# Attention's masked scores in the buffers of the recurrence's key and query copies, the output parts and their turned form in one block product buffer

## The chip, the cores and the metric

The kernel runs on one core of one Trainium2 chip. The metric is the device time of one execution in microseconds (us). The executions of the kernel before took 1199.67, 1202.01 and 1202.31 us; their median is 1202.01 us. A separate, profiled execution gave the trace that is read below.

The core has five engines that run at the same time, each through its own list of instructions in order: TensorE (PE, matrix products, with its weight loads as PEld), VectorE (DVE), ScalarE (ACT), GpSimd (POOL) and SyncE (SP, which here only issues DMA transfers). An instruction that must wait holds up everything behind it in its engine's list.

## What is computed

The reference is one decoder block over 1024 tokens of width 1024. A normalised input is projected by one wide matrix; the columns feed a gated linear recurrence (8 heads), a sliding-window attention (16 query heads in 4 groups, one key/value head for each group, window 128, with a sink logit in the denominator), two gates and two merge gates. Both branches are projected, merged, projected once more, added to the input and normalised. The change lies in the attention:

```python
scores = jnp.einsum('bnqhgd,bnkhd->bnhgqk', qb, keys).astype(jnp.float32) * (ATT_HEAD_DIM ** -0.5)
scores = jnp.where(valid[None, :, None, None], scores, -jnp.inf)
m = jnp.maximum(jnp.max(scores, axis=-1, keepdims=True), sink)
p = jnp.exp(scores - m)
probs = p / (jnp.sum(p, axis=-1, keepdims=True) + jnp.exp(sink - m))
out = jnp.einsum('bnhgqk,bnkhd->bnqhgd', probs.astype(v.dtype), vals)
```

## The kernel before

Every product runs on PE in 16-bit halves: an operand is split into a high and a low part (hi, lo), and a product is three passes, hi by hi, hi by lo and lo by hi. So a tile that feeds PE is written twice: ACT writes the high part, DVE the low one. Weights come in blocks of 256 columns. A block is loaded by SP into `raw` (L167, 1 MB, two buffers), DVE finds its largest magnitude (`wmx`, L205), ACT writes the high part `wh` (L236) and DVE the low part `wl` (L237), and PE multiplies (`mm_T`, L303; 24 products of 512 columns a tile of the result).

The attention runs in four rounds, one for each key/value head. A round begins with a weight block for the queries: PE makes `paq`, ACT and DVE write its two parts into `qs` (L762, L763). Then eight blocks of 128 tokens pass through stages that a generator (`attend`) starts three steps apart:

- scores: PE multiplies keys and queries into two PSUM banks `as` (L792)
- mask: DVE takes each of four heads, adds the mask, and writes the result to `sp` with the row maximum `amx` (L806); three small operations follow (L810 to L812)
- exps: ACT makes the exponentials in place in `sp` (L816, L820) and the high part `ph` (L823)
- turn: DVE writes the low part of `ph` (L827), SP transposes `ph` into `pT` by DMA (L832), DVE finishes the denominator `adn` (L833 to L835)
- values: PE multiplies `pT` with the values into `pv` (L842)
- divide: DVE makes the output `ao` (L852), ACT its high part in `ohl` (L859)
- back: DVE writes the low part of `ohl` (L862), SP transposes it into `aot` by DMA (L864)
- keep: DVE adds the two turned parts into the stored output `oaT` (L869), of which a later gate reads

Other weight blocks are worked off between the stages: the merge gates (`pm`), the attention's gates (`pg`, with `sg`, `gz` on L497 and L498, and the product `oaT` by `gz` on L918), and the projection of the recurrence's branch.

The lists of the engines aren't written by hand. A scheduler lays them out from the program's order, its own estimate of durations, and the buffers: a tile comes from a pool with a fixed number of buffers, and an operation that takes a tile when all are in use has to stand behind the release of the oldest. Three pools matter. `slot` is a pool of 24 buffers of 4 KB a partition that the attention's `sp`, `ph`, `pT`, `qs`, `kk`, `va`, `oaT` and others share. `tiny` holds small kinds: `kq` with three buffers (the recurrence's key and query copies, and `ohl`), and `hp` with two (the recurrence's block products, and `aot`). The recurrence has ended when the attention begins, so in the attention `kq` holds `ohl` alone and `hp` holds `aot` alone.

Of the kernel before, what the change touches and what calls it, by code (L numbers as in the profile page):

```python
# [14 lines left out]
F32 = mybir.dt.float32  # L15
F16 = mybir.dt.float16
# [7 lines left out]
P = 128  # L24
# [25 lines left out]
def phys(n):  # L50

    return n // 2 if n % 2 == 0 else 4 + n // 2
# [8 lines left out]
def view(ap, off, dims):  # L61

    base = ap[:, off : off + 1]
    return bass.AP(tensor=base.tensor, offset=base.offset, ap=[base.ap[0]] + dims)
# [3 lines left out]
def hybrid_block(ctx: ExitStack, tc: _tile.TileContext, x, norm_w, w_in, hlb, hnw, wbh, sinks, wba, w_out, fnw, out):  # L68
# [6 lines left out]
    tiny = ctx.enter_context(tc.tile_pool(name="tiny", bufs=4))  # L75
# [5 lines left out]
    def nm(s):  # L81
        uid[0] += 1
        return f"{s}{uid[0]}"

    def slot(name, shape=None, dt=F32):
        return sl.tile(shape or [P, 1024], dt, tag="s4", name=nm(name))

    def small(name, w, dt=F32, bufs=4):
        return tiny.tile([P, w], dt, tag=f"{name}_{w}", name=nm(name), bufs=bufs)

    def bank(name, pool=None):
        pool = pool or sm
        return pool.tile([P, HALF], F32, tag="bk", name=nm(name))
# [678 lines left out]
    def attention(r, qs, qsc):  # L772

        oaT[2 * r], oaT[2 * r + 1] = slot("oaT"), slot("oaT")
        sk = snk[:, 4 * r : 4 * r + 4]

        class Q:


            def __init__(self, n):  # L780
                self.n, self.own = n, phys(n)
                self.kbs = [self.own] if n == 0 else sorted([self.own, phys(n - 1)])
                self.nk = P * len(self.kbs)

            def scores(self):
                step = P * (self.kbs[-1] - self.kbs[0]) or P
                self.ps = [bank("as"), bank("as")]
                for i in range(4):
                    a, e = divmod(i, 2)
                    dst = self.ps[a][:, e * 256 : e * 256 + self.nk].rearrange("p (b k) -> p b k", k=P)  # L790
                    for w in range(2):
                        PE.matmul(  # L792
                            dst,
                            qs[a][:, e, self.own * P : (self.own + 1) * P],
                            view(kk[r][:, w], self.kbs[0] * P, [[step, len(self.kbs)], [1, P]]),
                            start=(w == 0),
                            stop=(w == 1),
                        )

            def mask(self):  # L800
                nk = self.nk
                self.mx, self.nm, self.es, self.dn = (small(x, 4) for x in ("amx", "anm", "aes", "adn"))
                self.s = slot("sp", [P, 4, 256])
                for i in range(4):
                    a, e = divmod(i, 2)
                    V.tensor_tensor_reduce(  # L806
                        self.s[:, i, 0:nk], self.ps[a][:, e * 256 : e * 256 + nk], amask[:, self.n % 2, 0:nk], qsc[:],
                        NEG, ALU.add, ALU.max, self.mx[:, i : i + 1],
                    )
                V.tensor_tensor(self.mx[:], self.mx[:], sk, ALU.max)  # L810
                V.tensor_scalar(self.nm[:], self.mx[:], -1.0, None, ALU.mult)  # L811
                V.tensor_tensor(self.es[:], sk, self.mx[:], ALU.subtract)  # L812

            def exps(self):
                for i in range(4):
                    A.activation(  # L816
                        self.s[:, i, 0 : self.nk], self.s[:, i, 0 : self.nk], AF.Exp, bias=self.nm[:, i : i + 1],
                        accum_out=self.dn[:, i : i + 1],
                    )
                A.activation(self.es[:], self.es[:], AF.Exp)  # L820
                self.p = slot("ph", [P, 2048], F16)
                self.hl = self.p[:, 0 : 8 * self.nk].rearrange("p (w i k) -> p w i k", w=2, i=4)
                A.activation(self.hl[:, 0], self.s[:, :, 0 : self.nk], AF.Copy, scale=2.0**14)  # L823

            def turn(self):

                V.scalar_tensor_tensor(  # L827
                    self.hl[:, 1], self.s[:, :, 0 : self.nk], 2.0**14, self.hl[:, 0], ALU.mult, ALU.subtract
                )
                self.pT = slot("pT", [P, 16, P], F16)  # L830
                nb = len(self.kbs)
                SP.dma_start(self.pT[:, 0 : 8 * nb], self.p[:, 0 : 8 * self.nk], transpose=True)  # L832
                V.tensor_tensor(self.dn[:], self.dn[:], self.es[:], ALU.add)  # L833
                V.reciprocal(self.dn[:], self.dn[:])
                V.tensor_scalar(self.dn[:], self.dn[:], 2.0**-14, None, ALU.mult)  # L835

            def values(self):
                self.pv = bank("pv")
                terms = [(b, pi, vi) for b in range(len(self.kbs)) for pi, vi in PASSES]
                for i in range(4):  # L840
                    for t, (b, pi, vi) in enumerate(terms):
                        PE.matmul(  # L842
                            self.pv[:, i * DH : (i + 1) * DH],
                            self.pT[:, (4 * pi + i) * len(self.kbs) + b],
                            va[vi][:, self.kbs[b], r * DH : (r + 1) * DH],
                            start=(t == 0),
                            stop=(t == len(terms) - 1),
                        )

            def divide(self):  # L850
                self.o = tiny.tile([P, 256], F32, tag="ao", name=nm("ao"), bufs=2)[:]
                V.tensor_tensor(  # L852
                    self.o.rearrange("p (i d) -> p i d", i=4),
                    self.pv[:, 0:256].rearrange("p (i d) -> p i d", i=4),
                    self.dn[:].rearrange("p (i o) -> p i o", o=1).broadcast_to([P, 4, DH]),
                    ALU.mult,
                )
                self.ohl = tiny.tile([P, 4, 256], F16, tag="kq", name=nm("ohl"), bufs=3)
                A.activation(self.ohl[:, 0], self.o, AF.Copy)  # L859

            def back(self):
                V.tensor_tensor(self.ohl[:, 1], self.o, self.ohl[:, 0], ALU.subtract)  # L862
                self.ot = tiny.tile([P, 8, P], F16, tag="hp", name=nm("aot"), bufs=2)
                SP.dma_start(self.ot[:, 0:4], self.ohl[:, 0:2].rearrange("p w d -> p (w d)"), transpose=True)  # L864

            def keep(self):
                for g in range(2):
                    dst = oaT[2 * r + g][:, self.own * P : (self.own + 1) * P]
                    V.tensor_tensor(dst, self.ot[:, g], self.ot[:, 2 + g], ALU.add)  # L869

        return [Q(n) for n in range(NB)]
# [398 lines left out]
    for n in range(2):  # L1270
        if n == 1:
            converts(n_out + 4)
        for tb in range(NB):
            half = tb // 4
            whole = n == 0 or tb < NB - 1
            for g in ((0, HALF),) if whole else ((0, 256), (256, HALF)):
                ps = bank("po", pj)
                t = 0
                for wi, ai in PASSES:
                    for k in range(KT):  # L1280
                        w = wout[n][wi][k * 2 // KT][:, k % (KT // 2), g[0] : g[1]]
# [59 lines left out]
```

## Time and profile before

| | us |
|---|---|
| median of three executions | 1202.01 (1199.67 to 1202.31) |
| the profiled execution | 1200.46 |
| its span, first instruction to last | 1198.8 |
| PE busy | 1150.4 (96%) |
| DVE busy | 860.6 (72%) |
| ACT busy | 527.1 (44%) |

The attention lies between 555 and 950 us of the span. Its rounds 0 and 1 end at about 640 and 720 us; between 720 and 800 us no attention block is at work; rounds 2 and 3 overlap and end at about 950 us. In the timeline, a figure in brackets behind an instruction is how long its engine stood idle just before it, and what ended that wait; an arrow `pT<-ph` reads "written from". Names are the program's, without buffer numbers.

### The profile page before, as it was taken

Reading aid. Unit: us, or ns where it says so; the run is one execution under the profiler, and the core shown is the slowest. Engines: PE = TensorE matmul, PEld = TensorE weight load, DVE = VectorE, ACT = ScalarE, POOL = GpSimd, SP = SyncE. Lnnn points to the kernel's source line nnn. Section 1 sums busy time; section 2 is a strip of 40 time slices with the busy share of each in tenths; the row PEclk is TensorE's granted clock in tenths of the full one; section 3 lists DMA queues with packets and bytes.
Section 4 is the critical chain, followed back from the end, with each engine's and each line's share of the span. In section 5 each row is a group of like instructions: output and inputs, shape, how many; then the busy total and the mean of one; then the engine's idle time right before and its main releaser. Section 6 shows DMA issues by size and latency. Waiting matters only on the chain.

```text
span 1198.8 us, 18078 instructions
## 1 busy us (share of the span) xinstructions
PE 1150.4 (96%) x7130; PEld 671.7 (56%) x7130; DVE 860.6 (72%) x2032; ACT 527.1 (44%) x1021; POOL 46.3 (4%) x96
## 2 busy tenths in 40 slices
PE   3999999999999999999999989999997999999997
PEld 3556687687688576574554544445454444444444
DVE  2887886895995996775777774259996877367645
ACT  2732532533433343353845761147778450223323
POOL 0240000000000000000000000000000000000000
PEclk8999999999999999999999999999999999999999
DMA  6121111111111111112562552124545412131312
GB/s 211 37 98 44 36 36 36 36 36 36 36 36 36 36 36 36 36 36 71 102 128 54 115 115 71 36 71 100 108 95 126 85 36 71 36 106 36 141 53 106
DMA packets 132646, 82.47 MB, mean 69 GB/s; under 512 B 81200, under 2 KB 129360, under 8 KB 132560
## 3 DMA queue, kind: packets, MB, share of 16 engines
q1 hardware_dynamic: 132560, 81.30, 24.7%
q8 instruction: 56, 0.92, 0.3%
q14 instruction: 30, 0.25, 0.1%
HBM read 57.17 MB, written 4.19 MB: 51 GB/s over the span
## 4 chain that ended last, share of the span: by engine, by line
PE 76%; DVE 10%; ACT 6%; DMA 5%; issue 2%; SPq 0%; POOL 0%; DVEq 0%; POOLq 0%; ACTq 0%
PE pm L303 19%; PE pg L303 11%; PE pv L315 7%; PE po L1282 7%; PE pq L303 7%; PE pf L303 5%; PE paq L303 5%; PE lv L613 3%; DMA pT<-ph 3%; ACT sp L816 2%; PE pk L303 2%; DVE ph L827 2%; DMA aot<-ohl 2%; PE pf L1129 1%; DVE sp L806 1%
## 5 line engine op out<-in xcount | busy, mean ns | idle before, releaser
L303 PEld LDWEIGHTS <-wh 128*128 128x128 f16 x2304 | 224.1, 98 | 256.9 <-issue 5.5
L303 PEld LDWEIGHTS <-wl 128*128 128x128 f16 x1152 | 112.7, 98 | 130.2
L236 ACT ACTIVATE wh<-raw,p_s 128x512 f16<-128x512 f32 x164 | 104.6, 709 | 117.3 <-issue 42.7
L237 DVE SCALAR_TENSOR_TENSOR wl<-raw,p_s,wh 128x512 f16<-128x512 f32 x164 | 114.1, 748 | 45.1 <-PE pm L303 18.6
L205 DVE TENSOR_REDUCE wmx<-raw 128x1 f32<-128x2048 f32 x45 | 102.6, 2281 | 47.0 <-DMA raw<-in_w_in_dram 25.2
L303 PE MATMUL pm<-hl,wh 128*128 128x512 f16 x512 | 117.0, 379 | 0.0
L1282 PE MATMUL po<-wo,hl 128*128 128x512 f16 (+1 forms) x408 | 83.1, 367 | 0.0
L816 ACT ACTIVATE sp<-sp,anm 128x256 f32<-128x256 f32 (+1 forms) x128 | 61.7, 483 | 24.5 <-DVE anm L811 24.0
L315 PEld LDWEIGHTS <-xh 128*128 128x128 f16 x640 | 62.7, 98 | 7.7
L1282 PEld LDWEIGHTS <-hl 128*128 128x128 f16 x408 | 39.9, 98 | 43.2
L303 PE MATMUL pg<-xl,wh 128*128 128x512 f16 x256 | 62.0, 379 | 0.0
L303 PE MATMUL pg<-xh,wh 128*128 128x512 f16 x256 | 60.8, 379 | 0.9 <-DVE qs L763 0.9
L303 PE MATMUL pm<-xh,wh 128*128 128x512 f16 x256 | 61.4, 382 | 0.0
L303 PE MATMUL pm<-xl,wh 128*128 128x512 f16 x256 | 61.3, 379 | 0.0
L303 PE MATMUL pg<-xh,wl 128*128 128x512 f16 x256 | 61.1, 379 | 0.0
L303 PE MATMUL pm<-xh,wl 128*128 128x512 f16 x256 | 60.7, 379 | 0.0
L303 PE MATMUL pm<-hl,wl 128*128 128x512 f16 x256 | 60.5, 379 | 0.0
L122 POOL PARTITION_ALL_REDUCE p_r<-wmx x47 | 26.6, 570 | 872.6 <-DVE wmx L205 656.3
L806 DVE CUSTOM_DVE_ANT_0 sp<-as,amask,qsc 128x256 f32<-128x256 f32 (+1 forms) x128 | 52.4, 463 | 3.8 <-DMA pT<-ph 3.5
L497 ACT ACTIVATE sg<-pg,wc 128x512 f32<-128x512 f32 x32 | 21.9, 683 | 47.0 <-PE pg L303 46.9
L315 PE MATMUL pv<-wh,xl 128*128 128x256 f16 x320 | 42.0, 273 | 0.0
L315 PE MATMUL pv<-wh,xh 128*128 128x256 f16 x320 | 41.6, 273 | 0.0
(219 smaller groups left out, 1921.7 us busy)
## 6 DMA issues: line engine op xcount, KB each, us to landing
raw<-in_w_in_dram SPq DMA_DIRECT2D x33, 1024.0 KB, 5.1
xt<-in_x_dram SPq DMA_DIRECT2D x8, 512.0 KB, 6.7
raw<-in_w_branch_hgrn_dram SPq DMA_DIRECT2D x4, 1024.0 KB, 5.2
raw<-in_w_branch_attn_dram SPq DMA_DIRECT2D x4, 1024.0 KB, 5.9
raw<-in_w_out_dram SPq DMA_DIRECT2D x4, 1024.0 KB, 5.1
xr<-in_x_dram SPq DMA_DIRECT2D x8, 512.0 KB, 8.3
out_dram<-xr SPq DMA_DIRECT2D x8, 512.0 KB, 2.6
raw<-in_w_in_dram SPq DMA_DIRECT2D x2, 512.0 KB, 4.1
```

Source lines behind the costliest of these rows:

```text
L122: last_all_max[0] = G.partition_all_reduce(r[:], mx, channels=P, reduce_op=bass_isa.ReduceOp.max)
L205: V.tensor_reduce(mx[:, j : j + 1], self.raw[:, ks], axis=AX.XY, op=ALU.max, apply_absolute_value=True)
L236: A.activation(hi, raw, AF.Copy, scale=s[:])
L237: V.scalar_tensor_tensor(lo, raw, s[:], hi, ALU.mult, ALU.subtract)
L303: PE.matmul(ps, w[:, k, ci * P : (ci + 1) * P], act(ai, k, t0, HALF), start=(n == 0), stop=(n == 3 * KT - 1))
L315: PE.matmul(ps, act(ai, k, t0, P), w[:, k, n0 : n0 + ncol], start=(n == 0), stop=(n == 3 * KT - 1))
L497: A.activation(sg[:], ps[:], AF.Sigmoid, scale=c[:])
L613: PE.matmul(lv[:, ms], kq[:, 0, ms], kq[:, 1, ms], start=True, stop=True)
L806: V.tensor_tensor_reduce(self.s[:, i, 0:nk], self.ps[a][:, e * 256 : e * 256 + nk], amask[:, self.n % 2, 0:nk], qsc[:], NEG, ALU.add, ALU. ...
L816: A.activation(self.s[:, i, 0 : self.nk], self.s[:, i, 0 : self.nk], AF.Exp, bias=self.nm[:, i : i + 1], accum_out=self.dn[:, i : i + 1],)
L827: V.scalar_tensor_tensor(self.hl[:, 1], self.s[:, :, 0 : self.nk], 2.0**14, self.hl[:, 0], ALU.mult, ALU.subtract)
L1282: PE.matmul(ps[:, g[0] : g[1]], mact(ai, k, tb * P, P), w, start=(t == 0), stop=(t == 3 * KT - 1))
```

## The change

`sp` is taken from `kq` (three buffers) and no longer from `slot`. `ohl` moves out of `kq`: `ohl` and the turned form become the two halves of one `hp` buffer (two buffers), taken at divide. `aot` is gone as a name; in the list of the changed kernel, the transposing DMA reads and writes a tile called `ohl`. The numbers and shapes of all operations stay as they are, apart from the loads of ACT's function tables, 39 before and 33 now. Lines behind the change shift by one or two (L862 becomes L864, L864 becomes L865, L869 becomes L870, L918 becomes L919).

```diff
--- before.py
+++ after.py
@@ -800,7 +800,7 @@
             def mask(self):
                 nk = self.nk
                 self.mx, self.nm, self.es, self.dn = (small(x, 4) for x in ("amx", "anm", "aes", "adn"))
-                self.s = slot("sp", [P, 4, 256])
+                self.s = tiny.tile([P, 4, 256], F32, tag="kq", name=nm("sp"), bufs=3)
                 for i in range(4):
                     a, e = divmod(i, 2)
                     V.tensor_tensor_reduce(
@@ -855,12 +855,13 @@
                     self.dn[:].rearrange("p (i o) -> p i o", o=1).broadcast_to([P, 4, DH]),
                     ALU.mult,
                 )
-                self.ohl = tiny.tile([P, 4, 256], F16, tag="kq", name=nm("ohl"), bufs=3)
+                both = tiny.tile([P, 2, 1024], F16, tag="hp", name=nm("ohl"), bufs=2)
+                self.ohl = both[:, 0].rearrange("p (w d) -> p w d", w=4)
+                self.ot = both[:, 1].rearrange("p (w q) -> p w q", w=8)
                 A.activation(self.ohl[:, 0], self.o, AF.Copy)
 
             def back(self):
                 V.tensor_tensor(self.ohl[:, 1], self.o, self.ohl[:, 0], ALU.subtract)
-                self.ot = tiny.tile([P, 8, P], F16, tag="hp", name=nm("aot"), bufs=2)
                 SP.dma_start(self.ot[:, 0:4], self.ohl[:, 0:2].rearrange("p w d -> p (w d)"), transpose=True)
 
             def keep(self):
```

Since a pool's buffers count in the scheduler's layout, the lists of all engines but POOL change. PE's is the same up to the end of round 1. There the last two values products stand 12 and 11 products of 512 columns earlier than before. In rounds 2 and 3, from the program's start to the last values product, there are 2797 products of 512 columns before and 2760 now; from the last scores product to the last values product, 116 before and 85 now. Of the 32 masks, 11 wait for a semaphore of a DMA before and none now; of the 32 writes of `ph` by ACT, 12 before and 18 now.

DVE at the end of round 0, in the list before (`ohl` on L862 is the low part of an output, `wmx` the search of a weight block, `qs` the low part of round 1's queries):

```order
L827 SCALAR_TENSOR_TENSOR ph_5809<-sp_5757,ph_5809 128x1024
L862 TENSOR_TENSOR ohl_5923<-ao_5921,ohl_5923 128x256
L205 TENSOR_REDUCE wmx_6362<-raw_6076 128x1
L763 SCALAR_TENSOR_TENSOR qs_5839<-paq_5841,qs_5839 64x512
L869 TENSOR_TENSOR oaT_5127<-aot_5865 128x128
L869 TENSOR_TENSOR oaT_5128<-aot_5865 128x128
L129 TENSOR_SCALAR p_r_6364<-p_r_6364 128x1
L763 SCALAR_TENSOR_TENSOR qs_5840<-paq_5910,qs_5840 64x512
L852 TENSOR_TENSOR ao_5984<-pv_5944,adn_5661 128x256
L130 TENSOR_SCALAR p_u_6366<-p_r_6364 128x1
L869 TENSOR_TENSOR oaT_5127<-aot_5934 128x128
L763 SCALAR_TENSOR_TENSOR qs_5839<-paq_5841,qs_5839 64x512
```

The same place in the list now:

```order
L827 SCALAR_TENSOR_TENSOR ph_5805<-sp_5753,ph_5805 128x1024
L835 TENSOR_SCALAR adn_5752<-adn_5752 128x4
L864 TENSOR_TENSOR ohl_5850<-ao_5848,ohl_5850 128x256
L763 SCALAR_TENSOR_TENSOR qs_5835<-paq_5837,qs_5835 64x512
L852 TENSOR_TENSOR ao_5916<-pv_5870,adn_5564 128x256
L763 SCALAR_TENSOR_TENSOR qs_5835<-paq_5837,qs_5835 64x512
L205 TENSOR_REDUCE wmx_6354<-raw_6068 128x1
L864 TENSOR_TENSOR ohl_5918<-ao_5916,ohl_5918 128x256
L870 TENSOR_TENSOR oaT_5127<-ohl_5850 128x128
L870 TENSOR_TENSOR oaT_5128<-ohl_5850 128x128
L129 TENSOR_SCALAR p_r_6356<-p_r_6356 128x1
L130 TENSOR_SCALAR p_u_6358<-p_r_6356 128x1
```

The search `wmx` stood ahead of all writes of `qs` shown; now two of these, of one half of the queries, stand ahead of it.

SP in round 1 (`pT` is the transpose that values waits for, `aot` and now `ohl` on L865 the transpose that keep waits for, `raw` a weight load), before:

```order
L832 DMA_TRANSPOSE pT_6560<-ph_6477 128x16x128
L864 DMA_TRANSPOSE aot_6607<-ohl_6586 128x4x128
L832 DMA_TRANSPOSE pT_6655<-ph_6570 128x16x128
L864 DMA_TRANSPOSE aot_6702<-ohl_6681 128x4x128
L167 DMA raw_7013<-in_w_branch_hgrn_dram 128x8x256
L832 DMA_TRANSPOSE pT_6750<-ph_6665 128x16x128
```

The same stretch now:

```order
L832 DMA_TRANSPOSE pT_6550<-ph_6468 128x16x128
L832 DMA_TRANSPOSE pT_6644<-ph_6560 128x16x128
L865 DMA_TRANSPOSE ohl_6576<-ohl_6576 128x4x128
L832 DMA_TRANSPOSE pT_6738<-ph_6654 128x16x128
L865 DMA_TRANSPOSE ohl_6670<-ohl_6670 128x4x128
L167 DMA raw_6997<-in_w_branch_hgrn_dram 128x8x256
```

The second `pT` shown stood behind an output transpose and now stands ahead of it; the third stood behind the weight load and now stands ahead of that.

DVE at the end of round 3, from the last block's mask to the last turn but one (L827), before:

```order
L833 TENSOR_TENSOR adn_8948<-adn_8948,aes_8947 128x4
L852 TENSOR_TENSOR ao_9209<-pv_9162,adn_8852 128x256
L498 SCALAR_TENSOR_TENSOR gz_9193<-pg_9128,cg_9124,sg_9194 128x512
L205 TENSOR_REDUCE wmx_9561<-raw_9367 128x1
L869 TENSOR_TENSOR oaT_8275<-aot_9152 128x128
L869 TENSOR_TENSOR oaT_8276<-aot_9152 128x128
L810 TENSOR_TENSOR amx_9040<-amx_9040,snk 128x4
L827 SCALAR_TENSOR_TENSOR ph_9001<-sp_8949,ph_9001 128x1024
```

Now, from behind the last turn but one to the weight search:

```order
L833 TENSOR_TENSOR adn_9015<-adn_9015,aes_9014 128x4
L834 RECIPROCAL adn_9015<-adn_9015 128x4
L835 TENSOR_SCALAR adn_9015<-adn_9015 128x4
L498 SCALAR_TENSOR_TENSOR gz_9164<-pg_9100,cg_9096,sg_9165 128x512
L919 TENSOR_TENSOR oaT_7541<-oaT_7541,gz_9164 128x512
L827 SCALAR_TENSOR_TENSOR ph_9068<-sp_9016,ph_9068 128x1024
L864 TENSOR_TENSOR ohl_9113<-ao_9111,ohl_9113 128x256
L852 TENSOR_TENSOR ao_9180<-pv_9133,adn_8826 128x256
L205 TENSOR_REDUCE wmx_9529<-raw_9335 128x1
```

The weight search `wmx` stood ahead of the last two turns and now stands behind both; on SP, the weight load that frees later in this round now stands right ahead of the last two `pT`.

## Rows read from the trace of the kernel before

**Rows 1.** the page's busy time: engine, us, share of the span, instructions

```profile
PE 1150.4 (96%) x7130; PEld 671.7 (56%) x7130; DVE 860.6 (72%) x2032; ACT 527.1 (44%) x1021; POOL 46.3 (4%) x96
```

**Rows 2.** busy us by stretch: PE, PEld, DVE, ACT, POOL, clock, DMA

```profile
555.00:642.00 87.00, 84.29 (x578) 43.77 (x577) 61.51 (x197) 54.95 (x126) 1.05 (x3) 0.98 0.44 95
642.00:720.00 78.00, 74.15 (x524) 38.40 (x523) 57.78 (x191) 51.79 (x118) 1.32 (x3) 1.00 0.48 105
800.00:860.00 60.00, 57.17 (x396) 30.54 (x394) 52.70 (x163) 45.52 (x106) 1.01 (x2) 1.00 0.43 93
860.00:950.00 90.00, 80.69 (x611) 42.73 (x609) 74.97 (x232) 65.13 (x141) 0.87 (x2) 0.98 0.54 115
...
898.90:926.80 27.90, 21.26 (x183) 11.70 (x181) 17.39 (x67) 22.67 (x53) 0.00 (x0) 0.94 0.58 117
```

**Rows 3.** PE's waits, rounds 0, 1, then 2 and 3: us, times, longest

```profile
PE paq L303 <- DVE qs L763: 1.8, 1, 1.8
PE pv L842 <- DMA pT<-ph: 0.9, 1, 0.9
...
PE pv L842 <- DMA pT<-ph: 2.4, 3, 1.1
PE pv L842 <- DVE ao L852: 1.4, 1, 1.4
...
PE pv L842 <- DMA pT<-ph: 8.8, 4, 3.3
```

**Rows 4.** PE's timeline at the end of round 0: start, us, instruction

```profile
632.05 3.42 PE L303 MATMUL paq<-xh,wh 128*128 128x512 f16 x8 [1.84 <-DVE qs L763]
635.30 1.89 PE L303 MATMUL paq<-xl,wh 128*128 128x512 f16 x8
637.03 1.89 PE L303 MATMUL paq<-xh,wl 128*128 128x512 f16 x8
```

**Rows 5.** DVE's timeline at the end of round 0

```profile
626.25 2.29 DVE L205 TENSOR_REDUCE wmx<-raw 128x1 f32<-128x2048 f32 x1 [1.21 <-DMA raw<-in_w_in_dram]
628.56 0.68 DVE L763 SCALAR_TENSOR_TENSOR qs<-paq,qs 64x512 f16<-64x512 f32 x1
```

**Rows 6.** SP's timeline in round 1: start, us, issue

```profile
692.01 1.65 SPq L864 DMA_TRANSPOSE aot<-ohl  x1
693.74 1.85 SPq L832 DMA_TRANSPOSE pT<-ph  x1
```

**Rows 7.** DVE's timeline in round 3

```profile
908.34 0.48 DVE L806 CUSTOM_DVE_ANT_0 sp<-as,amask,qsc 128x256 f32<-128x256 f32 x1 [1.01 <-DMA pT<-ph]
...
915.55 0.16 DVE L833 TENSOR_TENSOR adn<-adn,aes 128x4 f32<-128x4 f32 x1 [3.06 <-ACT aes L820]
...
926.43 0.49 DVE L869 TENSOR_TENSOR oaT<-aot 128x128 f32<-128x128 f16 x2 [2.46 <-DMA aot<-ohl]
...
927.18 0.48 DVE L806 CUSTOM_DVE_ANT_0 sp<-as,amask,qsc 128x256 f32<-128x256 f32 x1
...
930.06 2.28 DVE L205 TENSOR_REDUCE wmx<-raw 128x1 f32<-128x2048 f32 x1
```

**Rows 8.** DMA, us from issue to landing: median; then aot's min/median/max

```profile
raw<-in_w_in_dram SPq DMA_DIRECT2D x11, 1024.0 KB, 5.1
...
pT<-ph SPq DMA_TRANSPOSE x32, 4.3
...
DMA to landing us min/median/max: 2.4/3.0/5.8
```

**Rows 9.** attention stretch by line: busy us, mean ns, idle before

```profile
L869 DVE TENSOR_TENSOR oaT<-aot 128x128 f32<-128x128 f16 x60 | 15.3, 286 | 20.3 <-DMA aot<-ohl 16.6 <-DMA pT<-ph 3.5
...
L498 DVE SCALAR_TENSOR_TENSOR gz<-pg,cg,sg 128x512 f32<-128x512 f32 x13 | 9.7, 747 | 1.4 <-ACT sg L497 1.3
L918 DVE TENSOR_TENSOR oaT<-oaT,gz 128x512 f32<-128x512 f32 x12 | 8.2, 687 | 0.1
...
L816 ACT ACT_TABLE_LOAD x18 | 23.1, 1283 | 2.1 <-DVE aes L812 1.8
```

## Prediction before the run

> **What bounds the kernel now.** The first view is the page's busy time: PE is busy for 1150.4 of 1198.8 us [rows 1], so the kernel can only become faster by what PE loses, and the change takes no work from PE. The second is the busy time by stretch, to see where PE loses it. In the attention, 555 to 950 us, PE idles for 87.00 - 84.29 = 2.71 us in round 0, 3.85 us in round 1, and 2.83 + 9.31 = 12.14 us in rounds 2 and 3 [rows 2]. The same rows have the granted clock: 0.98 in the stretches 555 to 642 and 860 to 950, 1.00 in the others. One timeline shows what that costs: behind a wait of 1.84 us the next eight products took 3.42 us, the eight behind them 1.89 [rows 4], so 1.53 us were lost at the lower of the two levels. For the stretch to 950 us I take 2% of 90, 1.8 us. So the attention loses 4.2 us in round 0, 3.85 in round 1 and 12.1 + 1.8 = 13.9 in rounds 2 and 3: 22 us in all, and no change of the attention's order can bring much more.
>
> The third view, PE's waits, tells what ended these: `qs` of round 1's queries (1.8 us) and a `pT` (0.9) in round 0; three `pT` (2.4) and an `ao` (1.4) in round 1; in rounds 2 and 3 four `pT` (8.8, the longest 3.3) [rows 3]. The 9.31 us of 860 to 950 are nearly all `pT`; the 2.83 us of 800 to 860 have other causes, mainly the next queries' `qs`. The fourth view is DVE's timeline, for what delays `pT` and `qs`.
>
> **Round 0's end.** `wmx` stood idle 1.21 us for a weight load, ran 2.29 us, and only then came the `qs` that PE wanted [rows 5]. In the new list two `qs` stand ahead of it. That is 1.21 + 2.29 = 3.5 us earlier, more than the wait of 1.84 us, so this wait goes, and with it the 1.53 us of lower clock. The wait for `pT` of 0.86 us goes too if the values come where the transposes have long landed; the order leaves it as it was, so I give it a half chance, and since the clock may yet fall behind another wait, the bounds are 0 and -4.2. I take -1.84 - 1.53 - 0.43 = **-3.8**.
>
> **Round 1.** SP issued an `aot` at 692.01 and the next `pT` at 693.74 [rows 6]. In the new list that `pT` stands ahead of the output transpose, and the next stands ahead of the weight load. That is worth 1.7 us for one transpose, more than the longest `pT` wait of 1.1 us [rows 3]. Against that, the last two values stand 12 and 11 products earlier in PE's list, at (637.03 - 635.30)/8 = 0.216 us each [rows 4] 2.6 and 2.4 us of earlier need; but DVE's work ahead of the last two turns shrinks by some 4 us (an estimate from the instructions that no longer stand ahead of them at their mean durations). So the `pT` waits of 2.4 us go, and the `ao` wait of 1.4, which comes from PE's own values being divided late, may stay: bounds -1.1 and -3.85, taken **-2.4**.
>
> **Rounds 2 and 3: what goes.** 11 masks waited for a DMA and none does now. What one such wait costs DVE directly is small: one of 1.01 us is in round 3 [rows 7]. The bigger cost is the place: an operation that has to wait for a buffer is laid out late. The last mask starts at 927.18, behind a keep that had waited 2.46 us for its output transpose, and an `adn` had waited 3.06 us for ACT's exponentials, which came behind a table load [rows 7]. From 898.90 to 926.80 DVE is idle for 27.90 - 17.39 = 10.51 us [rows 2]. With `sp` out of the shared pool the masks of the last blocks stand 1 to 11.5 us of DVE work earlier, and six of 39 table loads of 1.283 us each [rows 9] are gone; I take 8 of the 10.5 us as recovered, with bounds of 0 and 10.5. Also, DVE has less to do ahead of the last turn: a `wmx` of 2.28 us [rows 7], a `gz` and its product with `oaT` (0.747 and 0.687 us) and two pairs of keeps at 0.286 us an instruction [rows 9], an `ao` and two low parts, 128x256 like a mask's 0.48 us [rows 7] and so some 0.4 each: 2.28 + 0.75 + 0.69 + 1.14 + 1.2 = 6.1 us of durations, which overlap by about a tenth, 5.4 is left.
>
> **Rounds 2 and 3: what comes.** The last values product stands 2797 - 2760 = 37 products earlier, 37 x 0.216 = 8.0 us, so PE asks for the last `pT` 8.0 us sooner. And the last two `pT` now follow a weight load on SP at once. Transposes of outputs landed 2.4 to 5.8 us after issue, 3.0 in the median [rows 8], so a bad place costs between 0 and 2.8 us; with 1 MB right ahead I take 2, near the late end. The Trainium skill, "DMA: Bandwidth & Descriptors", section "Queues, rings and completion order", states that each DMA engine consumes the descriptors of an issuing engine's ring in their order. By that the last `pT` would have to wait for the load's whole 1 MB, 5.1 us [rows 8] in place of 2, and the sum would be 3 us higher; the range below holds without it.
>
> The balance of what rounds 2 and 3 lose: 13.9 + 8.0 + 2 - 5.4 - 8 = 10.5 us in place of 13.9, so **-3.4**. With none of the idle recovered it is 18.5, +4.6. At the other end 10.5 us recovered and no late landing leave 6.0, -7.9, and below that stands 800 to 860 us with its 2.83 us, which the `qs` hold and the change doesn't touch.
>
> **The new tie.** An `hp` buffer is now held from divide to keep, and there are two. ACT's `ohl` of a block must wait for the keep of the block two before it. Behind `ohl` in ACT's list are exponentials, high parts and weights. From divide to keep it takes at least ACT's and DVE's parts (0.4 each), a landing of 3.0 us [rows 8] and two keeps (0.5), 4.3 us, while 16 blocks take the 150 us of 800 to 950, 9.4 us each, and keep has two blocks' time. I cost it at nothing; that cover is gone where keeps fall back behind other DVE work, as they do at 926.43. Six table loads less, 7.7 us of ACT, cost or bring nothing by themselves, since ACT is busy for 65.13 of 90 us in the tightest stretch [rows 2]. The Trainium skill, "ScalarE: Activation LUTs", section "What ACT_TABLE_LOAD costs", puts a switch at about 2.66 us with a drain; by that it would be 16 us of ACT, but the rows show 1.283 us and no drain behind it, so the row's price stands.
>
> **The sum** against the profiled execution's own time: 1200.46 - 3.8 - 2.4 - 3.4 = 1190.9. The median of the executions is 1.55 us above that one; a new median may lie as far above its own, so I add half of it and forecast **1191.5 us**, 0.9% faster.
>
> **Rivals.**
> 1. Nearly all goes (chance 0.14). With masks that never wait, each `pT` of rounds 2 and 3 lands before PE arrives; only the 2.83 us on `qs` and about 1 us stay. For it: the waits on `pT` are 8.8 of 12.1 us, and the values stand more evenly in PE's list. Against it: DVE and ACT already have 74.97 and 65.13 of 90 us of work there, and the need comes 8 us sooner. 1200.46 - 3.8 - 3.0 - 10 = 1183.7, and 1184.5 with the half of the median's distance.
> 2. The wait moves on (0.18). 24 buffers of the shared pool now serve `ph` and `pT` alone among the attention's short-lived tiles, but 18 writes of `ph` wait for a DMA where 12 did. Then ACT waits in the place of DVE, the turns come as late as before, and of rounds 2 and 3 only the 5.4 us against 8.0 + 2 remain: +4.6. With rounds 0 and 1 at -3.8 and -2.4: -1.6, 1198.9, 1199.7 on the median: within 0.2% or just faster.
> 3. The tie makes it slower (0.14). In round 3 ACT's `ohl` of each of the last eight blocks is held by a keep that waits for its output transpose; the longest such wait is 2.46 us [rows 7], and nine in the attention cost DVE 16.6 us [rows 9]. ACT then delays the exponentials of the next block, whose `pT` PE needs. Eight times 2.46 is 19.7 us, on top of the forecast 1211. It decides from about 10 us of such holds that reach PE; below that the kernel is still faster.
> 4. That the change does not do what it says is excluded by the order: no mask waits for a DMA any more.
>
> **How the numbers follow.** The forecast has 0.54, and its own range, from the bounds above, is 1186 to 1197. To leave out 2 in 10, the range reaches from 1183 (inside rival 1) to 1202 (the whole of rival 2), leaving out rival 3 and the tail of rival 1: **1183 to 1202**. A difference of about 0.2%, 2.4 us, is what a measurement of this kernel can tell from none. Faster by more than that: the forecast (0.54), rival 1 (0.14) and a third of rival 2 (0.06), 0.74. Within 0.2%: most of rival 2, 0.12. Slower: rival 3, 0.14.
>
> **What would show it.** In the new trace no mask waits for `pT`. At the end of round 0 PE's wait for `qs` and the eight slow products are gone; if it is still there, the search wasn't what delayed it. In round 1 the waits for `pT` are below 1 us together. In rounds 2 and 3, PE's waits for `pT` are fewer in the middle and the last one or two, behind the load, are 1 to 4 us long; DVE's idle time between the last scores and the last turn falls from 10.5 to about 2.5 us. If ACT's exponentials wait behind an `ohl` that waits for DVE's keep, rival 3 is at work; if `ph` waits for a DMA and the turns keep their distance, rival 2. The forecast is wrong if rounds 2 and 3 lose more than 17 us or if PE waits appear outside the attention.

## The result, and the profile after

The changed kernel took 1187.86 us in the median of four executions (1187.16 to 1189.14) beside 1201.93 us for the kernel before (1199.67 to 1202.31). The ratio is 0.9888 with a 95% interval of 0.9871 to 0.9905: it is faster by 1.1%, 14.1 us. The two profiled executions are only 11.3 us apart: that of before lies 1.5 us below its median, that of now 1.3 us above. Run once more beside the last experiments it took 1187.79 us, ratio 0.9896 (0.9877 to 0.9914).

The profiled execution took 1189.14 us, with a span of 1187.4; of before 1200.46 and 1198.8. The page's busy time, which answers [rows 1]:

```profile
PE 1147.2 (97%) x7130; PEld 670.7 (56%) x7130; DVE 859.2 (72%) x2032; ACT 518.4 (44%) x1015; POOL 45.4 (4%) x96
```

PE was idle for 1187.4 - 1147.2 = 40.2 us of the span and for 48.4 before, 8.2 us less; the other 3.2 us of the span are in PE's own busy time, which is longer at the lower clock (1.53 us of it are the eight slow products of [rows 4]). The same stretches as [rows 2] (stretch, its length, busy PE, PEld, DVE, ACT, POOL, clock, DMA share, GB/s):

```profile
555.00:642.00 87.00, 86.74 (x600) 45.41 (x597) 63.92 (x200) 54.93 (x126) 1.15 (x3) 1.00 0.43 95
642.00:720.00 78.00, 74.19 (x524) 38.76 (x525) 56.23 (x190) 48.93 (x116) 1.22 (x3) 1.00 0.51 105
800.00:860.00 60.00, 56.86 (x414) 30.92 (x413) 54.92 (x180) 45.88 (x113) 0.70 (x2) 1.00 0.51 111
860.00:950.00 90.00, 86.86 (x617) 44.55 (x615) 74.93 (x215) 57.22 (x127) 0.87 (x2) 0.98 0.54 107
```

The idle time of the first stretch has gone (2.71 to 0.26 us, and the clock from 0.98 to 1.00), that of the second has not moved (3.85 to 3.81), and the two of rounds 2 and 3 fell together from 12.14 to 6.28 us. PE's waits, which answer [rows 3], from 642 to 720 us and from 800 to 950 us (us in all, times, longest; from 555 to 642 us there is none):

```profile
PE pv L842 <- DMA pT<-ph: 2.1, 1, 2.1
PE as L792 <- DVE qs L763: 1.9, 2, 1.0
...
PE pv L842 <- DMA pT<-ph: 5.6, 5, 2.5
PE paq L303 <- DVE qs L763: 0.6, 1, 0.6
```

The wait of `paq` for `qs` at 632 us is gone. A wait of the scores `as` for later `qs` has come, 1.9 us at 642 to 645 us, so it belongs to the end of round 0 and only falls into the second stretch. In rounds 2 and 3 four waits for `pT`, two of them of 3.3 us, have given way to five of which two are over 1 us, and waits of 1.8 and 0.9 us for `qs` are gone.

Two marks cut the span where both lists of PE do the same: the first `paq` of round 1's queries, which PE makes at the end of round 0, and the first of round 2's. Before, then after (start, us, instruction):

```profile
611.36 1.89 PE L303 MATMUL paq<-xh,wh 128*128 128x512 f16 x8
...
779.58 1.89 PE L303 MATMUL paq<-xh,wh 128*128 128x512 f16 x8
```

```profile
610.97 1.89 PE L303 MATMUL paq<-xh,wh 128*128 128x512 f16 x8
...
774.51 1.89 PE L303 MATMUL paq<-xh,wh 128*128 128x512 f16 x8
```

From mark to mark, which is the end of round 0, round 1 and what lies up to round 2 (below: rounds 0 and 1), it took 168.22 us and takes 163.54 (-4.7); from there to the end 419.22 and 412.89 (-6.3). The 611 us ahead of the first mark, in which PE waits for nothing from 555 us on, differ by 0.4 us here, and by up to 3 us between the profiles of all kernels below, whose lists there are nearly the same. So kernels are compared by these two lengths, and by their medians.

### The profile page after: what moved, and what is told of

Its sections match the earlier page's. It is cut to its first block, busy times and chain, and to the rows that moved or that the text cites. A ratio compares the mean times of both kernels' runs of the same rounds, so it can differ in the third digit from the quotient of the medians.

```text
span 1187.4 us, 18078 instructions
## 1 busy us (share of the span) xinstructions
PE 1147.2 (97%) x7130; PEld 670.7 (56%) x7130; DVE 859.2 (72%) x2032; ACT 518.4 (44%) x1015; POOL 45.4 (4%) x96
## 4 chain that ended last, share of the span: by engine, by line
PE 77%; DVE 11%; DMA 6%; ACT 3%; issue 3%; POOL 0%; SPq 0%; ACTq 0%; DVEq 0%; POOLq 0%
PE pm L303 21%; PE pg L303 9%; PE pv L315 7%; PE po L1283 7%; PE pq L303 7%; PE pf L303 5%; PE paq L303 4%; PE lv L613 3%; DMA pT<-ph 2%; DMA raw<-in_w_in_dram 2%; PE pk L303 2%; DVE wl L237 2%; DVE sp L806 2%; PE pf L1130 1%; ACT sp L816 1%
## 5 line engine op out<-in xcount | busy, mean ns | idle before, releaser
L806 DVE CUSTOM_DVE_ANT_0 sp<-as,amask,qsc 128x256 f32<-128x256 f32 (+1 forms) x128 | 53.0, 463 | 0.8 <-PE as L792 0.5
```

The lines of the kernel that those rows point to most:

```text
L806: V.tensor_tensor_reduce(self.s[:, i, 0:nk], self.ps[a][:, e * 256 : e * 256 + nk], amask[:, self.n % 2, 0:nk], qsc[:], NEG, ALU.add, ALU. ...
```

## The experiments

The theory: the masks' place is what matters. As long as `sp` comes from a pool whose buffers other tiles hold until a transfer has landed, the layout puts masks late, and with them exponentials, turns and values. Rivals: the common buffer of `ohl` and the turned form brings the gain; fewer table loads do; more room for `ph` and `pT` in the shared pool does; or the layout merely fell out well.

| kernel | masks that wait for a DMA in the list | table loads | median us | rounds 0 and 1, mark to mark | from round 2 to the end |
|---|---|---|---|---|---|
| before | 11 | 39 | 1202 | 168.2 | 419.2 |
| changed | 0 | 33 | 1187.9 | 163.5 | 412.9 |
| changed, again (e9) | 0 | 33 | 1187.8 | 163.4 | 410.7 |
| sp alone (e1) | 6 | 33 | 1202.2 | 166.9 | 421.8 |
| common buffer alone (e2) | 10 | 39 | 1200.5 | 166.6 | 419.5 |
| before, search behind (e3) | 11 | 39 | 1200.3 | 165.6 | 420.8 |
| changed, three hp (e4) | 0 | 35 | 1194.7 | 164.8 | 414.5 |
| changed, third buffer of its own (e5) | 0 | 35 | 1192.9 | 162.4 | 415.8 |
| changed, keep on GpSimd (e6) | 0 | 35 | 1198.5 | 162.5 | 422.7 |
| changed, keep one step earlier (e7) | 0 | 33 | 1193.4 | 166.0 | 413.0 |
| before, keep one step earlier (e8) | 10 | 39 | 1204.4 | 169.8 | 419.8 |
| changed, keep behind qs (e10) | 0 | 35 | 1183.2 | 159.0 | 411.0 |
| changed, 23 slots (e11) | 0 | 33 | 1192.3 | 166.7 | 410.7 |
| changed, sp half in slot (e12) | 6 | 31 | 1207.5 | 174.7 | 420.2 |

### The two halves of the change

`sp` alone into `kq`, `ohl` and `aot` as before:

```diff
-                self.s = slot("sp", [P, 4, 256])
+                self.s = tiny.tile([P, 4, 256], F32, tag="kq", name=nm("sp"), bufs=3)
```

> Only the first half of the change: the masked scores sp go into kq, where the output parts ohl stay (three buffers for both); aot stays in hp. Theory: what matters is that the masks leave the shared pool, since then the layout puts masks, exponentials and turns earlier. In this kernel's list 6 masks still wait for a DMA (11 before, 0 with the whole change), there are 33 table loads as with the whole change, the two qs of round 1 stand ahead of the weight search, and the last values product stands 24 products of 512 columns earlier than before (37 with the whole change). So most of the gain of 14 us: 1190 to 1194 us. Rival, that the common buffer of ohl and aot brings the gain: 1200 to 1203 us.

The common buffer alone, `sp` as before:

```diff
-                self.ohl = tiny.tile([P, 4, 256], F16, tag="kq", name=nm("ohl"), bufs=3)
+                both = tiny.tile([P, 2, 1024], F16, tag="hp", name=nm("ohl"), bufs=2)
+                self.ohl = both[:, 0].rearrange("p (w d) -> p w d", w=4)
+                self.ot = both[:, 1].rearrange("p (w q) -> p w q", w=8)
...
-                self.ot = tiny.tile([P, 8, P], F16, tag="hp", name=nm("aot"), bufs=2)
```

> Only the second half of the change: ohl and the turned form share an hp buffer, sp stays in the shared pool. Theory: nothing is gained, since 10 masks still wait for a DMA, there are 39 table loads as before, and the weight search still stands ahead of the qs of round 1: 1200 to 1204 us. Rival, that the common buffer brings the gain: 1188 to 1193 us.

Measured: 1202.16 us, ratio 1.0002 (0.9992 to 1.0011), and 1200.52 us, ratio 0.9989 (0.9979 to 0.9999). Neither half brings the gain; the expectation for `sp` alone was wrong by some 10 us. The last values product stands 24 products earlier in its list than before (37 in the changed kernel), so an earlier place of the values alone brings nothing either. The trace of `sp` alone shows the new tie. ACT's waits from 800 to 950 us, then ACT, DVE and PE near 900 us:

```profile
ACT ohl L859 <- DMA aot<-ohl: 4.9, 3, 2.7
```

```profile
899.06 0.42 ACT L859 ACTIVATE ohl<-ao 128x256 f16<-128x256 f32 x1 [2.69 <-DMA aot<-ohl]
902.97 0.51 ACT L816 ACTIVATE sp<-sp,anm 128x256 f32<-128x256 f32 x1 [3.49 <-DVE anm L811]
```

```profile
898.49 2.27 DVE L205 TENSOR_REDUCE wmx<-raw 128x1 f32<-128x2048 f32 x1
...
902.77 0.16 DVE L811 TENSOR_SCALAR anm<-amx 128x4 f32<-128x4 f32 x1
```

```profile
910.50 1.86 PE L303 MATMUL pm<-xh,wh 128*128 128x512 f16 x4 [4.96 <-ACT sgm L973]
```

With `sp` and `ohl` in one pool of three buffers, ACT's next `ohl` waits until an older `ohl` has been transposed (2.69 us, 4.9 in all). The masks exchanged the release by `pT` for that by `aot`. PE's longest loss here, 4.96 us, is to a `sgm` that stands in ACT's list behind exponentials. These wait 3.49 us for `anm`, one of the small steps behind a mask; DVE, which was not idle, reached it at 902.77, with the weight search `wmx` ahead of that mask. So this loss comes from the place of the masks in DVE's list, and the wait of 2.69 us ahead of it didn't cause it. The second half of the change takes `ohl` out of `kq`; it pays only with the first, and the first only with it.

### Half of the masks in the shared pool

```diff
-                self.s = tiny.tile([P, 4, 256], F32, tag="kq", name=nm("sp"), bufs=3)
+                self.s = tiny.tile([P, 4, 256], F32, tag="kq", name=nm("sp"), bufs=3) if self.n % 2 else slot("sp", [P, 4, 256])
```

> The changed kernel with every second block's masked scores (even n) back in the shared pool, the others in kq. 6 masks wait for a DMA in its list, there are 31 table loads, the last values product stands 18 products earlier than before (37 with the whole change). If masks that wait for buffers are the cause, it lies between the two kernels: 1192 to 1199 us. If the number of ACT's table loads is the cause, it is as fast as the changed kernel: 1186 to 1190 us.

Measured: 1207.5 us, ratio 1.0061 (1.0041 to 1.0082): slower than either. It has the fewest table loads of all, 31, so these aren't the cause. That it is not between the two but behind both was expected by no theory. From round 2 on it takes 420.2 us, like the kernel before; what makes it the slowest lies in rounds 0 and 1 (174.7 us). PE's waits for `pT` in round 1 are twice those of before (2.4 us), and in rounds 2 and 3 as large (8.8):

```profile
PE pv L842 <- DMA pT<-ph: 5.0, 2, 4.5
...
PE pv L842 <- DMA pT<-ph: 9.0, 5, 5.1
```

### Is it room in the shared pool, or luck of the layout?

One buffer less in the shared pool of the changed kernel:

```diff
-    sl = ctx.enter_context(tc.tile_pool(name="sl", bufs=24))
+    sl = ctx.enter_context(tc.tile_pool(name="sl", bufs=23))
```

> The changed kernel with 23 buffers in the shared pool in place of 24. The masks stay free of DMA waits, but ph, pT and the others have one buffer less. If the gain comes from room in the shared pool that sp left to the others, a good part is lost: 1193 to 1199 us. If it comes from the masks' own freedom, the time stays with the family of the changed kernel: 1187 to 1193 us.

Measured: 1192.27 us, ratio 0.9933 (0.9913 to 0.9953). The median lies in the range of the masks' own freedom, near its end, and the lengths tell more: the part from round 2 on is as short as ever (410.7 us), and the loss is in rounds 0 and 1. So the part that the change won in rounds 2 and 3 doesn't hang on this one buffer. `sp` now uses three in `kq`, so the run tests only a part of that room, and no run gave the shared pool of the kernel before more buffers.

Keep one step earlier, in both kernels:

```diff
-    STAGES = {0: "scores", 1: "mask", 2: "exps", 5: "turn", 11: "values", 12: "divide", 13: "back", 18: "keep"}
+    STAGES = {0: "scores", 1: "mask", 2: "exps", 5: "turn", 11: "values", 12: "divide", 13: "back", 17: "keep"}
```

> The changed kernel with keep one step earlier in the program's order (17 for 18), an edit with no purpose of its own: it shows how far the time moves when the layout falls out another way. The list of PE differs from the changed kernel's in a few places of rounds 1 to 3. If the gain comes from the masks' freedom, the time stays near the changed kernel's: 1186 to 1191 us. If it is the luck of one layout, it may be anywhere up to 1200 us.

> The kernel before with the same edit, keep at step 17. 10 masks wait for a DMA in its list, the last values product stands 13 products later than before. If the lack of room for the masks is what costs: 1200 to 1205 us. If layouts differ by luck: it may be as low as 1190 us.

Measured: 1193.4 us, ratio 0.9927 (0.9911 to 0.9942), for the changed kernel and 1204.36 us, ratio 1.0023 (1.0013 to 1.0033), for the kernel before. An edit without a purpose makes the one slower by 5.5 us and the other by 2.6. So some of the 14 us may be good luck of the layout: with the edit the two kernels lie 11 us apart.

The last column of the table says it best. From round 2 on, seven of the eight rows in which no mask waits for a DMA have 410.7 to 415.8 us; the six in which masks do wait have 419.2 to 421.8. Those are profiles of single executions (e3, whose PE list is that of before, differs from before by 1.6 us there), but these groups don't overlap. The eighth row, keep on GpSimd, has 422.7 us and is the exception. The time doesn't grow with the number of waiting masks: with 6 it is 420.2 and 421.8 us, with 11 it is 419.2 and 420.8. In rounds 0 and 1 the groups overlap.

### The search at the end of round 0

The kernel before, with one edge: the weight search stands behind two `qs`, as in the changed kernel.

```diff
-                V.tensor_reduce(
+                with tc.issue_after(Block.held) if getattr(Block, 'held', None) and self.cols == MH + 512 else ExitStack(): V.tensor_reduce(
...
-                        V.scalar_tensor_tensor(
+                        held = V.scalar_tensor_tensor(
                             qs[a][other, e, sli], ps[rows], ZS, qs[a][rows, e, sli], ALU.mult, ALU.subtract
-                        )
+                        ); Block.held = getattr(held, "ins", held) if r == 1 and half + a == 0 else getattr(Block, "held", None)
```

> The kernel before, with one edge added: the weight search at the end of round 0 stands behind the two qs writes of round 1's first half, as it does in the changed kernel. The lists of PE and SP are those of before, DVE's differs in some 25 rows around that place. Theory of the prediction: PE's wait of 1.84 us for qs and the slow products behind it (1.53 us) go, 3.4 us: 1198.5 us, if no later qs takes its place. Rival, that the search only stood where DVE had to wait anyway: 1201 to 1203 us.

Measured: 1200.33 us, ratio 0.9989 (0.9979 to 0.9998), 1.7 us with an interval from 0.2 to 2.5. The search did hold PE, since the wait of `paq` is gone, but the gain is half of the 3.4 us. DVE after the search, then PE:

```profile
637.96 0.49 DVE L869 TENSOR_TENSOR oaT<-aot 128x128 f32<-128x128 f16 x2 [2.46 <-DMA aot<-ohl]
638.37 2.73 DVE L237 SCALAR_TENSOR_TENSOR wl<-raw,p_s,wh 128x512 f16<-128x512 f32 x4
641.13 0.69 DVE L763 SCALAR_TENSOR_TENSOR qs<-paq,qs 64x512 f16<-64x512 f32 x1
```

```profile
641.88 0.39 PE L792 MATMUL as<-kk,qs 128*128 128x256 f16 x2 [0.57 <-DVE qs L763]
643.80 0.39 PE L792 MATMUL as<-kk,qs 128*128 128x256 f16 x2 [0.89 <-DVE qs L763]
```

The last `qs` now come late, behind a keep that waits 2.46 us for its transpose, and PE gives back 1.46 us. The changed kernel has the same, with 1.9 us.

### Keeps out of the way of qs, and the new tie

Two experiments give the pair of `ohl` and turned form a third buffer, so that ACT waits for a keep one block later. In the first, all `hp` have three buffers and the gates' `sg` three instead of four; in the second, every third block has a buffer of its own:

```diff
-        sg = half_tmp("sg", bufs=4)
+        sg = half_tmp("sg", bufs=3)
...
-                both = tiny.tile([P, 2, 1024], F16, tag="hp", name=nm("ohl"), bufs=2)
+                both = tiny.tile([P, 2, 1024], F16, tag="hp", name=nm("ohl"), bufs=3)
```

```diff
-                both = tiny.tile([P, 2, 1024], F16, tag="hp", name=nm("ohl"), bufs=2)
+                both = tiny.tile([P, 2, 512], F16, tag="hq", name=nm("ohl"), bufs=1) if self.n % 3 == 2 else tiny.tile([P, 2, 1024], F16, tag="hp", name=nm("ohl"), bufs=2)
...
```

> The changed kernel with three hp buffers instead of two, so that ACT's ohl of a block waits for the keep of the block three before it; for the room, the gates' sg has three buffers instead of four, which alone leaves the lists of PE and SP as they are. In the changed kernel's trace ACT waited 1.8 us for keeps in all. If the tie of two buffers costs time: 1186 to 1187 us. If it costs nothing, as the prediction had it: 1187 to 1190 us.

> The changed kernel with a third buffer for the pair of output parts and turned form, for every third block, in room of its own (2 KB a partition, half of an hp buffer is all that the pair uses), with nothing taken from the gates' sg. The keeps stand as early in DVE's list as in the changed kernel. If the tie of two buffers costs time, 1184 to 1186.5 us; if not, 1186.5 to 1190 us. If the three-buffer run before (1194.7 us) was slow because of the third hp buffer itself and not because of the sg buffer taken away, 1192 to 1196 us.

Measured: 1194.71 us, ratio 0.9945 (0.9931 to 0.9959), and 1192.88 us, ratio 0.9921 (0.9905 to 0.9938). Both are slower than the changed kernel. The first is not a clean test, since ACT's `sg` waited 4.6 us for a buffer there:

```profile
ACT sg L974 <- DVE mg L976: 4.6, 1, 4.6
```

The second takes nothing from others, and is 5 us slower all the same, within what a purposeless edit does. Its time lies where its expectation put a cost of the third buffer itself, but with that spread the run can't tell. ACT waits for no keep in either; the 1.8 us of the changed kernel are gone, and no gain shows. So a third buffer is no remedy, and that the tie costs time isn't shown.

Keeps on GpSimd:

```diff
-                    V.tensor_tensor(dst, self.ot[:, g], self.ot[:, 2 + g], ALU.add)
+                    G.tensor_tensor(dst, self.ot[:, g], self.ot[:, 2 + g], ALU.add)
```

> The changed kernel with the keeps (64 additions of 128x128) on GpSimd in place of VectorE. Theory: with the new layout it is DVE's waits for the turned output in front of keep (16.6 us in the attention) that hold the qs at the end of round 0 and cost PE 1.9 us there; they leave DVE, and 1.9 to 5 us are gained: 1183 to 1186 us. Rival: GpSimd's additions, not priced in any trace here, and its changes between these and the weights' maxima delay the weight blocks: slower than 1190 us.

Measured: 1198.48 us, ratio 0.9971 (0.9959 to 0.9983), the rival's side. Rounds 0 and 1 are a little shorter (162.5 us), but rounds 2 and 3 lose, where PE waits 11.2 us for `pT`. Two delays are in the trace: one keep takes twice as long as on DVE (287 ns), and DVE's scale waits once for GpSimd's maximum. Which of them, if not the new layout, makes `pT` late isn't shown (POOL from 555 to 950 us, then DVE's waits from 800 to 950 us):

```profile
L870 POOL TENSOR_TENSOR oaT<-ohl 128x128 f32<-128x128 f16 x64 | 35.6, 581 | 122.8 <-DMA ohl<-ohl 69.0 <-issue 30.1 <-DMA pT<-ph 8.6
```

```profile
DVE p_r L129 <- POOL p_r L122: 4.3, 1, 4.3
```

Keeps on DVE, but in round 0 behind the `qs` that was written last in the program's order:

```diff
-                    V.tensor_tensor(dst, self.ot[:, g], self.ot[:, 2 + g], ALU.add)
+                    with tc.issue_after(Block.held) if r == 0 else ExitStack(): V.tensor_tensor(dst, self.ot[:, g], self.ot[:, 2 + g], ALU.add)
```

(`Block.held` is every write of `qs` on L763, the last one so far.)

> The changed kernel itself once more, beside the three below: 1186.5 to 1190 us. In the profiles so far the first 611 us, whose lists are nearly the same, took up to 3 us more or less from run to run; this run is the measure for the others.

> The changed kernel with edges on DVE: a keep of round 0 stands behind the qs write that the program issued last before it, so that its wait for the turned output no longer holds the qs of round 1. PE's list is the same. Theory: the two waits of 2.5 us in front of keeps at the end of round 0 are what makes PE wait 1.9 us for qs; 1.5 to 2 us are gained against the changed kernel beside it. Rival, that the wl writes of a weight block ahead of the last qs (2.7 us) hold them anyway: within 0.7 us of it.

Measured: 1183.22 us (1183.10 to 1184.52) beside 1187.79 us (1187.11 to 1189.78) for the changed kernel; ratios to before 0.9857 (0.984 to 0.9875) and 0.9896. It beats both kernels, by 4.6 us where 1.5 to 2 were expected. PE's list is unchanged; ACT's has two more table loads (35). DVE at the end of round 0 in the changed kernel, then with the edge:

```profile
633.38 0.49 DVE L870 TENSOR_TENSOR oaT<-ohl 128x128 f32<-128x128 f16 x2 [2.47 <-DMA ohl<-ohl]
...
635.97 0.42 DVE L864 TENSOR_TENSOR ohl<-ao,ohl 128x256 f16<-128x256 f32 x1
638.86 0.49 DVE L870 TENSOR_TENSOR oaT<-ohl 128x128 f32<-128x128 f16 x2 [2.46 <-DMA ohl<-ohl]
639.27 2.73 DVE L237 SCALAR_TENSOR_TENSOR wl<-raw,p_s,wh 128x512 f16<-128x512 f32 x4
642.04 0.69 DVE L763 SCALAR_TENSOR_TENSOR qs<-paq,qs 64x512 f16<-64x512 f32 x1
```

```profile
634.97 0.49 DVE L870 TENSOR_TENSOR oaT<-ohl 128x128 f32<-128x128 f16 x2
...
636.61 2.74 DVE L237 SCALAR_TENSOR_TENSOR wl<-raw,p_s,wh 128x512 f16<-128x512 f32 x4 [0.19 <-ACT wh L236]
639.38 0.69 DVE L763 SCALAR_TENSOR_TENSOR qs<-paq,qs 64x512 f16<-64x512 f32 x1
```

The `qs` comes at 639.38 and not at 642.04, though this execution reached the first mark 1.9 us later. PE waits for nothing from 555 to 720 us:

```profile
642.00:720.00 78.00, 78.00 (x546) 40.95 (x545) 54.54 (x183) 49.90 (x116) 1.22 (x3) 1.00 0.51 112
```

The changed kernel beside it waited only for `qs` there:

```profile
PE as L792 <- DVE qs L763: 2.6, 2, 1.7
```

All of the gain lies in rounds 0 and 1: 163.4 us in that execution and 159.0 now. Of these 4.4 us, 2.6 are the waits for `qs`, more than the 1.9 of the first profile; the rest is in PE's own busy time from mark to mark (160.8 and 159.0 us), since the granted clock from 642 to 660 us was 0.91 behind those waits and is 1.00 now. The expectation had left out the clock. ACT pays for it: from 600 to 660 us its `ohl` waits for keeps, by the tie, and PE doesn't notice:

```profile
ACT ohl L861 <- DVE oaT L870: 8.7, 3, 6.1
```

## Why the prediction held, step by step

The forecast was 1191.5 us with a range of 1183 to 1202; 1187.86 is inside, 3.6 us below. The sign, and the places where PE lost time, were right. Half of the 3.6 us isn't in the terms: their sum was 1190.9 us for a profiled execution, and that took 1189.14; the 0.6 us added for the median went the wrong way, as the new median lies 1.3 us below its profile. Misses of the terms also have opposite signs and cancel in part, and an edit without a purpose moves this kernel by 5.5 us, so that the sum came so near is partly luck. The terms:

- **Round 0's end** (-3.8). The wait for `qs`, the slow products and the wait for `pT` are gone, as costed (the `pT` whole, where half was taken), and e3 confirms that the search was the cause of the first. The step that fell short is "so this wait goes, and with it the 1.53 us of lower clock", which named no successor: the later `qs`, held by keeps that wait for their transposes, gave 1.9 us back, 2.6 in the second profile. In the list, behind the stretch that is shown, the last keeps of the round stand right behind the low part whose transpose they read (the trace has one at 635.97 and 638.86, above), and the median landing of 3.0 us [rows 8] was enough to see it.
- **Round 1** (-2.4). The first three waits for `pT` and the `ao` wait went, one of 2.14 us came; in the second profile of the same kernel there was none. So the sign that these waits stay below 1 us together was met by one of the two. Rounds 0 and 1 together brought 4.7 and 4.8 us in the two profiles, 6.2 predicted.
- **Rounds 2 and 3** (-3.4). Measured -6.3 and -8.5. Two terms were mis-sized. First, the idle time of DVE: from the first mask to the end of the last turn DVE was idle for 136.48 - 114.86 = 21.6 us and is for 120.40 - 108.10 = 12.3, 9.3 us less, where the sum took 8. The 10.5 us that it took them from lie ahead of the last mask, and not between the last scores and the last turn, as the prediction has it: in the 27.9 us that end there, DVE's idle time did fall to 2.5 us, while from the last scores to the last turn it was 5.5 and is 5.8. From the first mask to the last turn, before and then after:

```profile
804.07:940.55 136.48, 125.03 (x919) 66.95 (x918) 114.86 (x375) 104.45 (x235) 1.89 (x4) 0.99 0.50 107
```

```profile
799.00:919.40 120.40, 116.05 (x874) 62.70 (x873) 108.10 (x365) 96.48 (x227) 1.57 (x4) 1.00 0.59 119
```

Second, the two `pT` behind the weight load. The chain at the end of round 3 in the changed kernel (start, us, what):

```profile
906.16 5.42 DMA pT<-ph
...
912.65 6.43 DMA pT<-ph
919.08 0.05 issue
919.13 0.41 PE pv L842 x9
919.54 4.28 DMA pT<-ph
923.82 0.05 issue
923.87 1.02 PE pv L842 x24
```

The `pT` behind the load took 6.43 us, 2.1 more than the last one, so the 2 us that I took were near the price. How much of them is the load's isn't certain, since the `pT` at 906.16, with no load ahead, took 5.42 us. But PE had other products to do and lost 0.16 us on it, and the last `pT` left only when its turn had ended, with no load right ahead; its wait of 1.9 us is DVE's:

```profile
919.13 0.87 PE L842 MATMUL pv<-va,pT 128*128 128x64 f16 x24 [0.16 <-DMA pT<-ph]
...
923.87 1.02 PE L842 MATMUL pv<-va,pT 128*128 128x64 f16 x24 [1.93 <-DMA pT<-ph]
```

So this term was nearly nothing on the path. With 9.3 for 8 and nothing for 2, the prediction's balance gives -6.7. SP's issue of the `pT` behind the load, and the load itself, issued at 911.49 (the last figure is the us to its landing):

```profile
912.65 4.43 SPq L832 DMA_TRANSPOSE pT<-ph  x1
```

```profile
raw<-in_w_branch_attn_dram SPq DMA_DIRECT2D x1, 1024.0 KB, 5.7
```

By the Trainium skill, "DMA: Bandwidth & Descriptors", "Queues, rings and completion order", each DMA engine consumes descriptors in the order of their ring, so those of a load that stand ahead are consumed first. The trace agrees: SP was held by that issue until 917.08, the load landed at 917.2, and the `pT` 1.9 us behind it. Its price is still 2.1 us and not the load's whole 5.1, which I gave as what the rule would make of it, since the load was already under way and a `pT` takes 4.3 us without one.

- **The tie** was costed at nothing. That held: in the changed kernel ACT waited 1.8 us for keeps in the attention, with the edge of e10 8.7 us from 600 to 660 alone, with no cost to PE there. The changed kernel, from 555 to 950 us:

```profile
ACT ohl L861 <- DVE oaT L870: 1.8, 2, 1.0
```

- **The rivals.** The result lies halfway between the forecast and "nearly all goes" (1184.5), but that rival's mechanism, that each `pT` of rounds 2 and 3 lands before PE arrives, didn't come: PE still waits 5.6 us for them. e10 comes as low by rounds 0 and 1 and not by these. "The wait moves on" was for `ph`: 18 of its writes can wait for a DMA in the list, but in the trace ACT waits for none. In e1 the waits did move, to `aot`. The tie didn't make it slower.
- **Table loads** were said to bring nothing by themselves, and e12, with the fewest and the longest time, agrees.

The direct waits of masks (`sp` on L806) were only 3.5 us in the trace of before, of which 1 in round 3; in the changed kernel what is left is a wait for the scores. How long the engines stood idle ahead of work on `sp`, and until what (us, times), before and then after:

```profile
  DMA pT<-ph: 3.5, 3
```

```profile
  PE as L792: 0.5, 1
```

So most of the gain is not theirs. That it comes through the order that the layout can choose when masks are free is borne out for rounds 2 and 3 by the two groups of the table, with one exception, and not for rounds 0 and 1; which change of the order brings it isn't isolated. What stays open: how much of the 14 us is luck; whether more buffers in the shared pool would have done the same; and why half of the masks in each pool is worse than all in either.

## What to carry to other kernels

A tile that a scheduler could place freely is worth taking out of a pool whose other tiles are held until a transfer has landed, if the new pool has no such tiles either: here the move brought nothing without the second half, which emptied the new pool. After a stall is removed, read the in-order list for the next instruction that waits for a transfer on the same engine; one edge that put such waiters behind the work PE wants gave another 4.6 us. And run one or two purposeless edits before crediting a layout's gain to a cause.

## What the runs showed of the hardware

The additions of 128x128 from 16-bit halves took 581 ns on GpSimd and 287 ns on DVE. A transpose issued 1.2 us behind a 1 MB load held SP for 4.43 us and landed after 6.43, where the median of its kind is 4.3; with no load ahead one took 5.42. The first 611 us took up to 3 us more or less between the profiles of these kernels, whose lists there are nearly the same, and 1.2 us between two of the changed kernel, so stages are better compared from mark to mark than from the start.
